# Output weights split during the value projection and kept in DRAM in parts; zero matmuls first, first tokens in halves on two queues

## The chip, the core and the metric

The kernel runs on one core of a Trainium2 chip. TensorE (PE) multiplies, ScalarE (ACT) and VectorE (DVE) work on tiles, GpSimd (POOL) does a few masks and starts some transfers, SyncE (SP) starts most transfers. The metric is the device time of one execution in microseconds, the median of three timed runs. 0.2% of it is 2.1 us.

## The reference

One layer of a decoder on 1024 tokens of width 1024, all in float32, where `P`, `q`, `k`, `v` and `f` are column groups of one projection:

```python
h = x @ w_in                                   # columns [pool 512 | q 512 | k 512 | v 512 | gate 8]
pool = scale * GroupLinear(TrailingMean_w(u) - u)        # 4 groups of 128 channels, w = 2, 4, 8, 16
attn = softmax(q k^T / 8 + c_t - c_s, causal) v          # 8 heads of 64, c = cumsum(log sigmoid(f + b_f))
x = LayerNorm(alpha * x + concat(pool, attn) @ w_out)    # w_out is 1024 x 1024
x = LayerNorm(alpha * x + relu(x @ w_mlp1)**2 @ w_mlp2)  # hidden width 4096
```

## The kernel before

Every float32 operand of a product is kept as two parts: `hi`, a copy rounded to the type that PE multiplies in one pass (a CAST on ACT, line 71), and `lo`, what the rounding left (a subtraction on DVE, line 72). `split` (lines 70 to 72) makes both. A product is three matmuls, hi by hi, hi by lo and lo by hi (`three`, lines 83 to 85).

The program is one straight list for each engine; every engine takes its own list in order, and a planner that works with estimated durations sets that order when the program is built. Buffers are slots of five pools in on-chip memory (S for raw input, Q and A for general use, B for long-lived operands, U for small ones), and a slot that is taken again waits for its last reader. On-chip sums lie in eight banks named `s`, `pt`, `pv` and `mm`. A transfer is started by the engine in whose list it stands; if it has to wait, all that stands behind it on that engine waits too.

The stages in order of time:

- Value projection, to about 54 us. x comes transposed: `load_x(c, kp)` loads and splits 256 input channels of token half c. `load_wvf(kp)` does the same for the value and gate weights. For the first 512 tokens the loop runs over the eight channel blocks k outside and over 8 banks inside, so PE starts as soon as block 0 is there; for the second 512 tokens each of 8 (token tile, column half) pairs runs over all k. `vf_out` copies a finished bank out (line 157 on ACT, 158 and 160 on DVE).
- Pooling and query/key projections from the same x tiles (`load_w`, `proj`, `pool_group`, `qk_proj`), then attention over 8 heads in 4 pairs (`att_probs`, `att_values`). The next pair's projection is fed into attention piece by piece as filler; in the last pair the filler is pooling group 0 (`last_fill`), whose result goes through a DRAM scratch `mix_dram`, as the heads' results do.
- Output projection from about 315 us: `wout` is loaded to S slots and split into B slots (the loop before `load_row`, line 482), which come free when the x tiles are done, that is, while the last pair of heads runs. Its other operand is read back from `mix_dram` (line 750).
- Layer norm, the two products of the MLP with a two-level Strassen scheme, layer norm.

Of the kernel before, what the change touches and what calls it, by code (L numbers as in the profile page):

```python
# [8 lines left out]
F32 = mybir.dt.float32  # L9
# [5 lines left out]
P = 128  # L15
# [21 lines left out]
def trunk(ctx, tc, xT, xn, wuqk, wvf, bf, poolw, pscale, wout, g1, b1, w1, w2, g2, b2, out):  # L37
# [70 lines left out]


    xs = {}  # L110

    def load_x(c, kp):
        st = slot("Q" if c == 0 else "S", [2, CH], F32)
        for k in range(2):
            if c == 0 and kp == 0:
                nc.sync.dma_start(st[:, k], xT[c, kp, :, k])
            elif k == 0:
                nc.sync.dma_start(st, xT[c, kp])
            if k == 0:
                x = slot("B", [2, 2, CH])  # L120
            t = x[:, k]
            split(t[:, 0], t[:, 1], st[:, k])
            xs[c, 2 * kp + k] = t

    wv = []

    def load_wvf(kp):
        st = slot("S", [2, 2 * VW], F32)
        hi, lo = slot("A", [2, 2 * VW]), slot("A", [2, 2 * VW])
        wv.append((hi, lo))  # L130
        if kp:
            nc.sync.dma_start(st, wvf[kp])
        for k in range(2):
            pieces = [slice(0, VW), slice(VW, 2 * VW)] if kp == 0 and k == 0 else [slice(0, 2 * VW)]
            for c in pieces:
                if kp == 0:
                    nc.sync.dma_start(st[:, k, c], wvf[kp, :, k, c])
                split(hi[:, k, c], lo[:, k, c], st[:, k, c])
                yield
# [21 lines left out]

    for kp in range(4):
        g = load_wvf(kp)
        if kp == 0:
            next(g)
        load_x(0, kp)
        for _ in g:
            pass
    nc.sync.dma_start(bf_sb, bf)
    nc.sync.dma_start(ps_sb, pscale)  # L170
    acc0 = []
    for t in range(4):
        acc0.append(tuple(bank()[:, 0:VW] for _ in range(2)))
# [7 lines left out]
    for kp in range(4):  # L181
        load_x(1, kp)
    for t in range(4, NT):
        for half in range(2):
            b = bank()[:, 0:VW]
            for k in range(KT):
                vf_mm(t, half, b, k)
            vf_out(t, half, b)

# [288 lines left out]
    for kp in range(KT // 2):  # L478
        hi, lo = slot("B", [2, D]), slot("B", [2, D])
        for k in range(2):  # L480
            st = slot("S", [D], F32)
            nc.sync.dma_start(st, wout[2 * kp + k])
            split(hi[:, k], lo[:, k], st)
            wo.append((hi[:, k], lo[:, k]))
# [667 lines left out]
```

## Time and profile before

| | us |
|---|---|
| three timed runs | 1046.09, 1044.00, 1045.35 |
| their median | 1045.35 |
| the profiled execution, whole | 1042.84 |
| its span, first to last instruction | 1041.1 |
| PE busy in the span | 1014.8 |
| DVE busy | 760.5 |
| ACT busy | 510.1 |

PE is busy for 97% of the span; the other engines have room on average. What stays is to ask where PE is not busy, or busy and slow, and which instruction ended each wait. Times below are counted from the span's start.

### The profile page before, as it was taken

The page shows a single profiled execution, that of the slowest core. Times are in us where ns is not written, and L with a number is a line of the kernel's source. Part 1 is how long each engine was busy: PE and PEld are TensorE (multiplying, and loading weights), DVE is VectorE, ACT ScalarE, POOL GpSimd, SP SyncE. Part 2 cuts the span into 40 slices and gives each one's busy share as a digit, 9 for nine tenths or more (in the row PEclk, how much of TensorE's full clock was granted, in tenths as well). Part 3 has the DMA queues.
Part 4 walks back from the last instruction along what each step waited for, and adds up shares of the span by engine and source line. Part 5 has one row for each costly group of instructions (what it writes and reads, how often), then busy time and mean ns, then how long its engine had stood idle before and what let it go on. Part 6 is the DMA issues. An engine that isn't in the chain of part 4 may idle for free.

```text
span 1041.1 us, 13988 instructions
## 1 busy us (share of the span) xinstructions
PE 1014.8 (97%) x4958; PEld 842.8 (81%) x4958; DVE 760.5 (73%) x1301; ACT 510.1 (49%) x819; POOL 137.2 (13%) x236
## 2 busy tenths in 40 slices
PE   8999999999989999999999999999999999999996
PEld 7988888878767888888888888888788888888885
DVE  4576678777795896989887878788875565566547
ACT  4423566666674331677666766768621121122152
POOL 0000112111000021113112122120100000000047
PEclk9999999999999999999999999999999999999998
DMA  6302311111346542139757667565999888878753
GB/s 224 104 28 82 103 51 52 34 49 55 113 151 178 194 148 95 62 120 362 286 223 272 233 246 279 215 263 188 342 314 312 273 267 285 277 223 272 237 190 122
DMA packets 111798, 195.81 MB, mean 188 GB/s; under 512 B 9256, under 2 KB 77672, under 8 KB 111728
## 3 DMA queue, kind: packets, MB, share of 16 engines
q1 hardware_dynamic: 95600, 136.71, 40.1%
q0 software_dynamic: 15840, 57.68, 14.3%
q8 instruction: 39, 0.64, 0.2%
q10 hardware_dynamic: 288, 0.52, 0.1%
q14 instruction: 31, 0.25, 0.1%
HBM read 127.18 MB, written 67.70 MB: 187 GB/s over the span
## 4 chain that ended last, share of the span: by engine, by line
PE 52%; DVE 5%; DMA 1%; issue 0%; ACT 0%; POOL 0%; DVEq 0%; SPq 0%
PE s L953 15%; PE s L599 9%; PE pv L953 8%; PE pt L599 6%; PE mm L599 6%; PE pv L599 4%; PE pt L953 2%; PE mm L953 2%; DVE B L72 1%; DVE A L722 1%; DMA hid_dram<-A 1%; DMA A<-hid_dram 1%; DVE Q L72 0%; DMA S<-in_w_dram 0%; DVE bns L502 0%
## 5 line engine op out<-in xcount | busy, mean ns | idle before, releaser
L71 ACT CAST B<-S 128x1024 fp32r<-128x1024 f32 (+1 forms) x92 | 78.3, 870 | 171.9 <-DMA S<-in_w_dram 66.4
L72 DVE TENSOR_TENSOR B<-S,B 128x1024 fp32r<-128x1024 f32 (+1 forms) x92 | 90.2, 993 | 35.1 <-ACT B L71 35.0
L599 PE MATMUL s<-B,Q 128*128 128x512 f32 x480 | 113.5, 389 | 0.2 <-ACT B L71 0.2
L599 PEld LDWEIGHTS s<-B,Q 128*128 128x128 f32 x480 | 90.0, 188 | 19.3 <-ACT B L71 0.6
L953 PE MATMUL s<-B,Q 128*128 128x512 f32 x390 | 94.8, 389 | 0.0
L953 PEld LDWEIGHTS s<-B,Q 128*128 128x128 f32 x390 | 73.2, 188 | 15.5
L71 ACT CAST Q<-S 128x1024 fp32r<-128x1024 f32 x52 | 54.5, 1050 | 62.3 <-PE s L599 17.0
L953 PE MATMUL s<-B,A 128*128 128x512 f32 x333 | 83.1, 394 | 1.1 <-DMA A<-hid_dram 1.1
L724 POOL DMA_DIRECT2D hid_dram<-A x90 | 48.3, 541 | 219.0 <-ACT A L721 174.6
L953 PEld LDWEIGHTS s<-B,A 128*128 128x128 f32 x333 | 62.4, 188 | 15.8 <-DMA A<-hid_dram 1.7
L72 DVE TENSOR_TENSOR Q<-S,Q 128x1024 fp32r<-128x1024 f32 x52 | 63.2, 1216 | 12.1 <-ACT Q L71 12.0
L599 PE MATMUL pt<-B,Q 128*128 128x512 f32 x300 | 71.6, 389 | 0.0
L599 PE MATMUL mm<-B,Q 128*128 128x512 f32 x300 | 71.6, 389 | 0.0
L391 PE MATMUL pv<-A,B 128*128 128x256 f32 x320 | 62.8, 298 | 6.7 <-ACT A L376 3.8
L391 PEld LDWEIGHTS pv<-A,B 128*128 128x128 f32 x320 | 49.9, 188 | 22.3 <-ACT A L376 11.1
L599 PEld LDWEIGHTS mm<-B,Q 128*128 128x128 f32 x300 | 56.3, 188 | 11.7
L599 PEld LDWEIGHTS pt<-B,Q 128*128 128x128 f32 x300 | 56.3, 188 | 11.7
L377 DVE TENSOR_TENSOR A<-pt,A 128x512 fp32r<-128x512 f32 (+1 forms) x80 | 49.0, 633 | 15.8 <-ACT A L376 15.3
L355 ACT ACTIVATE A<-A,nm 128x1024 f32<-128x1024 f32 (+7 forms) x64 | 49.7, 776 | 18.8 <-DVE nm L353 17.5
L722 DVE TENSOR_TENSOR A<-A,A 128x1024 f32<-128x1024 f32 x45 | 53.6, 1219 | 0.8 <-ACT A L721 0.8
L340 POOL TENSOR_TENSOR A<-A,maskb 128x128 f32<-128x128 f32 x48 | 22.4, 467 | 232.9 <-DVE nm L353 135.7
L953 PE MATMUL pv<-B,Q 128*128 128x512 f32 x204 | 50.2, 389 | 0.0
(401 smaller groups left out, 2297.9 us busy)
## 6 DMA issues: line engine op xcount, KB each, us to landing
hid_dram<-A POOLq DMA_DIRECT2D x105, 512.0 KB, 4.0
S<-in_w_dram SPq DMA_DIRECT2D x62, 512.0 KB, 3.5
Q<-hid_dram SPq DMA_DIRECT2D x101, 256.0 KB, 4.7
A<-hid_dram SPq DMA_DIRECT2D x79, 256.0 KB, 5.3
S<-in_wuqk_dram SPq DMA_DIRECT2D x12, 512.0 KB, 3.3
A<-ncf_dram SPq DMA_DIRECT2D x8, 512.0 KB, 3.7
S<-in_wout_dram SPq DMA_DIRECT2D x8, 512.0 KB
S<-mix_dram SPq DMA_DIRECT2D x8, 512.0 KB, 5.0
```

The lines of the kernel that those rows point to most:

```text
L71: nc.scalar.copy(hi, src)
L72: nc.vector.tensor_tensor(lo, src, hi.bitcast(F32), ALU.subtract)
L340: nc.gpsimd.tensor_tensor(nb[:, qs], nb[:, qs], maskb, ALU.add)
L355: nc.scalar.activation(pt[:, :nk], pt[:, :nk], AF.Exp, bias=nm, scale=-1.0, accum_out=rsum[h][:, i : i + 1])
L377: nc.vector.tensor_tensor(tt[:, 1, ev], tp[:, ev], tt[:, 0, ev].bitcast(F32), ALU.subtract)
L391: nc.tensor.matmul(ov, V[j][:, h].rearrange("p s d -> p (s d)"), tt[:, s, a:b], start=(j == 0 and s == 0), stop=(j == 2 * m + 1 and s == 1),)
L599: nc.tensor.matmul(dst, b[x][:, k], A[a][y][:, k], start=first and k == 0 and i == 0, stop=k == H - 1 and i == 2, skip_group_check=not first,)
L722: nc.vector.tensor_tensor(x, x, hi.bitcast(F32), ALU.subtract)
L724: nc.gpsimd.dma_start(hid_dram[self.u, :, i, AT[name] : AT[name] + 2 * CH], part.rearrange("p q n t -> p (q n t)"))
L953: nc.tensor.matmul(dst, h[:, p_], w[q_], start=first and u == self.us[0] and j == 0, stop=u == self.us[-1] and j == 2, skip_group_check=no ...
```

## The change

Four things are edited.

- At the start 18 matmuls of 128 by 256 zeros are put ahead of PE's list (they write a bank that the first real product overwrites), after one MEMSET on DVE.
- The first x block is loaded in halves: its first 256 tokens are started from ACT's list, the rest from SP's. The first block of weights is loaded whole instead of in two column pieces, and weights and x now alternate. The loads of the second token half go to Q slots instead of S slots.
- In the value projection of the second token half, each of the 8 steps also loads one 128-row block of `wout`, splits it (CAST on ACT, line 199 of the new program; subtraction on DVE, line 200) and starts two transfers of 512 KB from POOL's list (line 202) that store `hi` and `lo` in a new DRAM scratch `wo_dram`.
- In front of the output projection the 8 loads of `wout` with 8 splits are replaced by 16 loads of the stored parts straight into the B slots (line 509), with no work on ACT or DVE.

```diff
--- before.py
+++ after.py
@@ -106,21 +106,25 @@
     rin_dram = dr.tile([NH, S], F32, name="rin_dram")
     mix_dram = dr.tile([4, P, 8, 256], F32, name="mix_dram")
 
+    wo_dram = dr.tile([KT, 2, P, D], F32, name="wo_dram")
+
 
     xs = {}
 
     def load_x(c, kp):
-        st = slot("Q" if c == 0 else "S", [2, CH], F32)
+        st = slot("Q", [2, CH], F32)
+        x = slot("B", [2, 2, CH])
+        if c or kp:
+            nc.sync.dma_start(st, xT[c, kp])
         for k in range(2):
-            if c == 0 and kp == 0:
-                nc.sync.dma_start(st[:, k], xT[c, kp, :, k])
-            elif k == 0:
-                nc.sync.dma_start(st, xT[c, kp])
-            if k == 0:
-                x = slot("B", [2, 2, CH])
             t = x[:, k]
-            split(t[:, 0], t[:, 1], st[:, k])
             xs[c, 2 * kp + k] = t
+            first = c == kp == k == 0
+            for i, r in enumerate((slice(0, 256), slice(256, CH)) if first else (slice(0, CH),)):
+                if c == kp == 0:
+                    (nc.scalar if first and i == 0 else nc.sync).dma_start(st[:, k, r], xT[c, kp, :, k, r])
+                split(t[:, 0, r], t[:, 1, r], st[:, k, r])
+                yield
 
     wv = []
 
@@ -131,10 +135,9 @@
         if kp:
             nc.sync.dma_start(st, wvf[kp])
         for k in range(2):
-            pieces = [slice(0, VW), slice(VW, 2 * VW)] if kp == 0 and k == 0 else [slice(0, 2 * VW)]
-            for c in pieces:
-                if kp == 0:
-                    nc.sync.dma_start(st[:, k, c], wvf[kp, :, k, c])
+            if kp == 0:
+                nc.sync.dma_start(st[:, k], wvf[kp, :, k])
+            for c in [slice(0, VW), slice(VW, 2 * VW)] if kp == 0 and k == 0 else [slice(0, 2 * VW)]:
                 split(hi[:, k, c], lo[:, k, c], st[:, k, c])
                 yield
 
@@ -159,18 +162,20 @@
         hs = slice(4 * half, 4 * half + 4)
         nc.vector.tensor_tensor(z[:, t, hs], src[:, 4 * HD : VW], bf_sb[:, hs], ALU.add)
 
+
+    acc0 = [tuple(bank()[:, 0:VW] for _ in range(2)) for t in range(4)]
+    zero = slot("Q", [256])
+    nc.vector.memset(zero.bitcast(F32), 0.0)
+    for _ in range(18):
+        nc.tensor.matmul(acc0[3][1][:, 0:256], zero[:, 0:P], zero, start=True, stop=True)
+
     for kp in range(4):
-        g = load_wvf(kp)
-        if kp == 0:
-            next(g)
-        load_x(0, kp)
-        for _ in g:
-            pass
+
+        gw, gx = load_wvf(kp), load_x(0, kp)
+        for g in (gw, gx, gw, gx, gw, gx):
+            next(g, None)
     nc.sync.dma_start(bf_sb, bf)
     nc.sync.dma_start(ps_sb, pscale)
-    acc0 = []
-    for t in range(4):
-        acc0.append(tuple(bank()[:, 0:VW] for _ in range(2)))
     for k in range(KT):
         for t in range(4):
             for half in range(2):
@@ -179,13 +184,35 @@
         for half in range(2):
             vf_out(t, half, acc0[t][half])
     for kp in range(4):
-        load_x(1, kp)
+        for _ in load_x(1, kp):
+            pass
+
+    raw = {}
+
+    def load_output_weights(k):
+        if k < KT:
+            raw[k] = slot("Q", [D], F32)
+            nc.sync.dma_start(raw[k], wout[k])
+
+    def split_output_weights(k):
+        hi, lo = slot("Q", [D]), raw[k]
+        nc.scalar.copy(hi, lo)
+        nc.vector.tensor_tensor(lo, lo, hi.bitcast(F32), ALU.subtract)
+        for i, part in enumerate((hi.bitcast(F32), lo)):
+            nc.gpsimd.dma_start(wo_dram[k, i], part)
+
+    AHEAD = 3
+    for k in range(AHEAD):
+        load_output_weights(k)
     for t in range(4, NT):
         for half in range(2):
             b = bank()[:, 0:VW]
             for k in range(KT):
                 vf_mm(t, half, b, k)
             vf_out(t, half, b)
+            k = 2 * (t - 4) + half
+            load_output_weights(k + AHEAD)
+            split_output_weights(k)
 
 
     zf = z.rearrange("p t h -> p (t h)")
@@ -478,9 +505,8 @@
     for kp in range(KT // 2):
         hi, lo = slot("B", [2, D]), slot("B", [2, D])
         for k in range(2):
-            st = slot("S", [D], F32)
-            nc.sync.dma_start(st, wout[2 * kp + k])
-            split(hi[:, k], lo[:, k], st)
+            for i, part in enumerate((hi, lo)):
+                nc.sync.dma_start(part[:, k].bitcast(F32), wo_dram[2 * kp + k, i])
             wo.append((hi[:, k], lo[:, k]))
 
     def load_row(tag, src):
```

The planner is run anew on the changed program. Its lists are the same as before (but for names) outside three places: the start, the value projection of the second token half, and the last pair of heads up to the first tiles of the output projection.

**PE, program start.** Before, PE's list began with the first product of the value projection (`A` is weights, `B` is x):

```order
L83 MATMUL s_166<-A_100,B_107 128x260 [waits Activation_49]
L84 MATMUL s_166<-A_101,B_107 128x260 [waits DVE_49]
L83 MATMUL s_168<-A_100,B_107 128x260
L85 MATMUL s_166<-A_100,B_107 128x260 [waits DVE_49]
L83 MATMUL pt_167<-A_100,B_107 128x260 [waits Activation_49]
L84 MATMUL s_168<-A_101,B_107 128x260
```

Now it begins with the 18 zero matmuls, and the first four products are hi by hi of two token tiles:

```order
L170 MATMUL mm_107<-Q_108 128x256 [waits DVE_49]
L170 MATMUL mm_107<-Q_108 128x256 x17
L83 MATMUL s_100<-A_129,B_135 128x260 [waits Activation_49]
L83 MATMUL s_102<-A_129,B_135 128x260
L83 MATMUL pt_101<-A_129,B_135 128x260 [waits Activation_49]
L83 MATMUL mm_103<-A_129,B_135 128x260
L84 MATMUL s_100<-A_130,B_135 128x260 [waits DVE_49]
L85 MATMUL s_100<-A_129,B_135 128x260
```

The zero matmuls wait for DVE's MEMSET alone; the first real matmul stands behind all 18.

**ACT, value projection of the second token half.** Before, the bank copies (line 157) followed the last x casts, with the weights of the next projection between them (line 71, `S` source):

```order
L71 CAST B_415<-S_413 128x512 [waits DMAHW0_49]
L71 CAST B_415<-S_413 128x512
L157 CAST B_445<-s_420 128x4x64 [waits PE_49]
L157 CAST B_445<-pt_449 128x4x64 [waits PE_49]
L157 CAST B_445<-s_477 128x4x64 [waits PE_49]
L157 CAST B_445<-mm_505 128x4x64 [waits PE_49]
L157 CAST B_558<-s_533 128x4x64 [waits PE_49]
L71 CAST B_678<-S_676 128x1024 [waits DMAHW1_49]
L71 CAST B_772<-S_770 128x1024 [waits DMAHW2_49]
```

Now seven CASTs of `wout` blocks (line 199) stand among the bank copies (line 160), and the next projection's weights stand behind them; `DMASW` is a wait for an earlier store started by POOL, because `hi` takes the slot that it left:

```order
L199 CAST Q_515<-Q_445 128x1024 [waits DMAHW2_49,DMASW0_49,DVE_49]
L199 CAST Q_550<-Q_447 128x1024 [waits DMAHW3_49,DVE_49]
L199 CAST Q_585<-Q_478 128x1024 [waits DMAHW4_49,DVE_49]
L160 CAST B_474<-s_449 128x4x64 [waits PE_49]
L199 CAST Q_621<-Q_513 128x1024 [waits DMAHW5_49,DMASW2_49,DVE_49]
L160 CAST B_474<-pt_485 128x4x64 [waits PE_49]
L199 CAST Q_654<-Q_548 128x1024 [waits DMASW3_49,DMAHW1_49,DVE_49,Activation_49]
L160 CAST B_474<-s_520 128x4x64 [waits PE_49]
L199 CAST Q_687<-Q_583 128x1024 [waits DMASW4_49,DMAHW2_49,DVE_49,Activation_49]
L199 CAST Q_720<-Q_619 128x1024 [waits DMAHW3_49,DMASW5_49]
L160 CAST B_474<-mm_555 128x4x64 [waits PE_49]
L160 CAST B_615<-s_590 128x4x64 [waits PE_49]
```

The eighth, of block 0, stands further up, ahead of the first bank copy. DVE's list has the eight subtractions in the matching places.

**DVE and SP, last pair of heads.** DVE before, at the end of pooling group 0 (lines 260 and 262, and line 72 with `Q` operands), with a split of `wout` (line 72, `B` from `S`) between:

```order
L260 SCALAR_TENSOR_TENSOR Q_3252<-Q_3249,Q_2935 128x1023 [waits DVE_49]
L262 TENSOR_TENSOR Q_3252<-Q_3252,Q_2935 128x1 [waits DVE_49]
L397 TENSOR_TENSOR U_3297<-pv_3231,U_3297 64x256 [waits DMAHW0_49,Activation_49]
L353 ISA A_3308,nm_3312<-s_3309,A_2862 128x512
L353 ISA nm_3312 128x1
L406 RECIPROCAL ri_3375<-rsum_2928 128x2
L72 TENSOR_TENSOR B_3561<-S_3562,B_3560 128x1024 [waits DMAHW7_49]
L72 TENSOR_TENSOR Q_3257<-Q_3252,Q_3256 128x1024 [waits Activation_49]
```

DVE now, at the same place:

```order
L287 SCALAR_TENSOR_TENSOR Q_3331<-Q_3328,Q_3014 128x1023 [waits DVE_49]
L289 TENSOR_TENSOR Q_3331<-Q_3331,Q_3014 128x1 [waits DVE_49]
L424 TENSOR_TENSOR U_3376<-pv_3310,U_3376 64x256 [waits DMAHW4_49,Activation_49]
L380 ISA A_3387,nm_3397<-s_3393,A_2941,nm_3391 128x384
L380 ISA nm_3397 128x1
L380 ISA A_3400,nm_3404<-s_3401,A_2941 128x512
L380 ISA nm_3404 128x1
L72 TENSOR_TENSOR Q_3336<-Q_3331,Q_3335 128x1024 [waits Activation_49]
```

The split is gone, and a softmax step (line 380) now stands ahead of the pooling group's split. On SP, before, the row of gate sums for the last head (`ncf_dram`, line 324) stood ahead of `wout` loads:

```order
L398 DMA mix_dram<-U_2907 64x256 [waits DMAHW1_49,DVE_49]
L411 DMA rin_dram<-row_2964 8x128 [waits DMAHW2_49,Activation_49]
L324 DMA A_2927<-ncf_dram 128x1024 [waits DMAHW3_49,PE_49]
L482 DMA S_3542<-in_wout_dram 128x1024 [waits DMAHW4_49,DVE_49]
L411 DMA rin_dram<-row_3013 2x128 [waits DMAHW5_49,Activation_49]
L482 DMA S_3546<-in_wout_dram 128x1024 [waits DMAHW6_49,DVE_49]
```

Now two loads of stored parts stand ahead of it (line 351 is the same load of the row):

```order
L425 DMA mix_dram<-U_2921 64x256 [waits DMAHW6_49,DVE_49]
L509 DMA B_3609<-wo_dram 128x1024 [waits DMAHW7_49,DMASW0_49,PE_49]
L509 DMA B_3609<-wo_dram 128x1024 [waits DMAHW0_49,DMASW2_49]
L425 DMA mix_dram<-U_2986 64x256 [waits DMAHW1_49,DVE_49]
L438 DMA rin_dram<-row_3043 8x128 [waits DMAHW2_49,Activation_49]
L351 DMA A_3006<-ncf_dram 128x1024 [waits DMAHW3_49]
L509 DMA B_3610<-wo_dram 128x1024 [waits DMAHW4_49,PE_49]
```

The first of the two waits for PE to release the slot and for POOL's store of that part.

## Rows read from the trace of the kernel before

**Rows 1.** The page, its part 1: busy time of each engine.
```profile
PE 1014.8 (97%) x4958; PEld 842.8 (81%) x4958; DVE 760.5 (73%) x1301; ACT 510.1 (49%) x819; POOL 137.2 (13%) x236
```

**Rows 2.** Busy time by stretch: engines, granted clock, DMA share, GB/s.
```profile
4.60:9.60 5.00, 4.71 (x19) 4.37 (x20) 2.80 (x5) 2.58 (x5) 0.00 (x0) 1.00 0.89 342
270.00:290.00 20.00, 19.69 (x119) 16.22 (x118) 17.88 (x48) 16.56 (x40) 1.25 (x4) 1.00 0.43 146
290.00:310.00 20.00, 15.66 (x96) 12.08 (x94) 18.69 (x42) 14.78 (x29) 0.62 (x2) 1.00 0.40 139
310.00:330.00 20.00, 17.40 (x107) 14.45 (x106) 13.98 (x25) 10.85 (x21) 0.62 (x2) 1.00 0.72 210
470.00:480.00 10.00, 9.67 (x44) 7.69 (x42) 9.79 (x13) 6.53 (x9) 4.32 (x8) 1.00 1.02 379
```

**Rows 3.** Timeline, first 11 us: start, duration, engine, line, operation [idle before, releaser].
```profile
0.74 0.20 POOL masks.py:197 MEMSET ident<- 128x128 f32 x1 [0.29 <-POOLq L1141]
...
4.64 0.59 PE L83 MATMUL s<-A,B 128*128 128x260 f32 x1 [4.64 <-ACT B L71]
...
7.35 0.63 ACT L71 CAST A<-S 128x520 fp32r<-128x520 f32 x1 [1.19 <-DMA S<-in_wvf_dram]
...
9.30 0.38 PE L85 MATMUL pt<-A,B 128*128 128x260 f32 x1
...
9.51 0.29 PE L83 MATMUL pv<-A,B 128*128 128x260 f32 x1
...
9.64 0.28 PE L84 MATMUL pv<-A,B 128*128 128x260 f32 x1
...
10.24 0.28 PE L83 MATMUL s<-A,B 128*128 128x260 f32 x1
```

**Rows 4.** Busy time of PE in the value projection, its two halves.
```profile
4.64:30.41 25.77, 25.51 (x192) 1.00 0.52 196
30.41:54.29 23.88, 23.69 (x194) 1.00 0.34 114
```

**Rows 5.** Groups of instructions from 255 to 310 us, by shape.
```profile
L72 DVE TENSOR_TENSOR B<-S,B 128x1024 fp32r<-128x1024 f32 x8 | 9.7, 1211 | 0.0
...
L71 ACT CAST B<-S 128x1024 fp32r<-128x1024 f32 x8 | 8.4, 1045 | 0.5 <-DMA S<-in_wout_dram 0.5
```

**Rows 6.** Waits of PE from 255 to 345 us.
```profile
PE pv L391 <- ACT A L376: 3.5, 4, 1.4
PE pv L391 <- DVE A L377: 1.9, 3, 1.0
PE mm L83 <- ACT Q L71: 1.3, 1, 1.3
```

**Rows 7.** Timeline, 294 to 316 us.
```profile
295.01 1.22 DVE L72 TENSOR_TENSOR B<-S,B 128x1024 fp32r<-128x1024 f32 x1
...
301.55 1.20 DVE L72 TENSOR_TENSOR B<-S,B 128x1024 fp32r<-128x1024 f32 x1
...
302.67 1.21 DVE L72 TENSOR_TENSOR Q<-Q,Q 128x1024 fp32r<-128x1024 f32 x1
...
303.93 0.50 PE L84 MATMUL mm<-Q,U 128*128 128x512 f32 x1 [0.92 <-DVE Q L72]
...
315.34 0.50 PE L83 MATMUL s<-B,Q 128*128 128x512 f32 x1
```

**Rows 8.** The page, its parts 2 and 6: mean DMA rate, issues to landing.
```profile
DMA packets 111798, 195.81 MB, mean 188 GB/s; under 512 B 9256, under 2 KB 77672, under 8 KB 111728
...
hid_dram<-A POOLq DMA_DIRECT2D x105, 512.0 KB, 4.0
```

**Rows 9.** Timeline, 270 to 278 us.
```profile
273.08 0.34 SPq L324 DMA_DIRECT2D A<-ncf_dram  x1
...
276.92 0.29 DVE L353 CUSTOM_DVE_ANT_0 A<-s,A 128x128 f32<-128x128 f32 x1 [0.15 <-DMA A<-ncf_dram]
```

**Rows 10.** Timeline, 45 to 50 us.
```profile
46.82 2.00 ACT L71 CAST B<-S 128x1024 fp32r<-128x1024 f32 x2
```

## The prediction

> **What bounds the kernel now.** I read the page's busy times first: PE is busy for 1014.8 us of a 1041.1 us span, no other engine above three quarters [rows 1]. So time can only be won where PE stands still, or runs at its lower clock level. The busy times by stretch came second, to find such places near the edits. Two stand out. From 4.6 to 9.6 us PE ran only 19 matmuls; from 290 to 330 us it was busy for 15.66 + 17.40 of 40 us, so 6.9 us idle, with DVE busy for 18.69 of the first 20 us [rows 2]. The timelines of these places came third, then what PE waited for.
>
> At the start PE's first matmul is at 4.64 us. Matmuls of 260 columns follow each other at 0.21 us up to 9.51 us (9.30 to 9.51), and at 0.12 us from there (9.64 to 10.24 is five of them) [rows 3]. 260 columns in 0.21 us is the 1.2 GHz level, in 0.12 us the 2.4 GHz level. So the clock rose 4.9 us after PE began, and channel block 0 took from 4.64 to 10.24 us: 5.6 us, where 24 matmuls at 0.12 us take 2.9. After that PE never starves in the first half: it ends at 30.41 us [rows 4].
>
> Beside this stands the granted clock of the same stretch, 1.00 [rows 2], which would say that PE ran at full speed all along. The Trainium skill ("TensorE: Matmul & The Clock Gate", section "Seeing it yourself") warns that the clock events in a trace have been seen to be unreliable. By the column the zeros could win nothing and would only delay the first product (rival B); by the spacing they win the term below. The spacing is measured on the matmuls themselves, so it decides.
>
> At the end of attention PE waits for ACT's casts of turned probabilities (3.5 us), for DVE's subtractions of them (1.9) and for the split of pooling group 0 (1.3 and, at 303.93, 0.9 us) [rows 6, 7]. The splits of `wout` stand in these two lists: 8 casts of 1.05 us on ACT and 8 subtractions of 1.21 us on DVE between 255 and 310 us [rows 5].
>
> **The change part by part.** The sum is made against the profiled execution, 1042.84 us, of which 1.7 us lie outside the span; it is 2.5 us below the median of 1045.35, and I take the difference over to the median.
>
> *Zeros.* DVE fills the tile as soon as the engines start: 0.74 us, plus at most twice POOL's 0.20 us for half as many elements [rows 3], so PE begins at about 1.2 us. 18 matmuls of 256 columns at 0.21 us are 3.9 us, to 5.1 us. If the clock again rises 4.9 us after PE's first matmul, that is at 6.1 us. Block 0 then runs from 5.1: 5 matmuls slow to 6.1, 19 at 0.12 us, done at 8.4 us instead of 10.24. That is a gain of 1.8 us, if block 1 is there. Its last cast began at 7.35 and took 0.63 us [rows 3], so it was ready at 7.98 with the same 1 MB loaded ahead of it as now; the new alternation of weights and x does not make it later. Bounds: with the clock up at 5.1 us block 1's data is the limit, a gain of 2.3; with no effect of the zeros on the clock a loss of 0.5, since the first product starts at 5.1 instead of 4.64 us.
>
> *Halves on two queues, whole weight block.* About the same bytes have to land before the first product as before, and PE is in the zeros until 5.1 us. Cost and gain nothing beside the zeros. If the cover goes (data later than 5.1 us), each microsecond costs one, up to the 2.5 us or so by which block 1 could slip.
>
> *x of the second half in Q slots.* These loads no longer wait for S slots. The second half of the value projection took 23.88 us [rows 4] where 192 matmuls at 0.12 us are 23.0. I take 0.5 of the 0.9 us, since the first x cast still stands behind the fifth bank copy; bounds -0.3 (one more such wait) and +0.9.
>
> *Splits moved into the value projection.* 8 casts of 1.05 and 8 subtractions of 1.21 us, 8.4 and 9.7 us, now lie between about 20 and 46 us. PE waits for none of them. What stands behind them is the bank copies (each bank is needed again only by the next projection, after 52 us) and the casts of that projection's weights, which ran at 46.82 us before [rows 10] and are needed by about 52. The new waits are ACT's casts that wait for a store from POOL to leave its slot. A store of 512 KB landed 4.0 us after its issue [rows 8]. The last such wait is for the store of block 1's `lo`, issued at about 36.5 us (my estimate: x casts done at about 33, three casts, then DVE), so at about 41 us; only a landing after some 47 us would reach PE. Cost zero, bounds 0 and +3 us if stores run at half that speed with queues. On SP the loads of the next weights stand behind `wout` loads that wait for slots, with the same margin. POOL has nothing else to do here.
>
> *Splits gone from the end of attention.* Here the gain lies on the chain of pooling group 0: its split feeds the products at 303.93 us, whose result goes to DRAM and back before the output projection can begin at 315.34 us [rows 7]. Two `wout` subtractions stand in DVE's list ahead of that split, at 295.01 and 301.55 us, 1.22 and 1.20 us [rows 7]; without them the chain comes 2.4 us sooner, and the output projection with it. I take 2.4 us. What is late next is the latency from transposed probabilities over ACT and DVE back to PE, 3.5 + 1.9 us of waits [rows 6], which shrinks only in part. Bounds: all 6.9 us of idle time, and a loss of 1.4 us, the longest single wait there [rows 6], since the planner set PE's list anew and gives the last heads fewer output matmuls as filler.
>
> *16 loads instead of 8.* 8.4 MB instead of 4.2 MB pass while the last pair of heads runs. 270 to 310 us moved 146 and 139 GB/s, 5.7 MB; now about 10 MB, 250 GB/s, where 470 to 480 us reached 379 GB/s [rows 2]. It fits, with no cost on the sum. Two of these loads stand ahead of the gate-sum row of the last head, which was issued at 273.08 us and for which DVE waited 0.15 us at 276.92 [rows 9]; at 379 GB/s they put it off by up to 2.8 us. DVE has two splits less there, PE was busy for 19.69 of 20 us with filler at hand [rows 2], so I count zero, bound 1.5.
>
> Sum: 1.8 + 0.5 + 2.4 = 4.7 us. 1042.84 - 4.7 = 1038.1 for a profiled execution, 1045.35 - 4.7 = 1040.6 us for the median. After 330 us the lists are unchanged and PE is the bound, so a gain is kept.
>
> **The rivals.**
>
> A. *The end of attention gains nothing.* The chain of pooling group 0 gives way, but the in-order waits for turned probabilities take its place. For it: 5.4 of 7.6 us of waits there are of that kind, and PE gets less filler. Against: the same two engines get 18 us lighter. Time 1045.35 - 2.3 = 1043.05.
>
> B. *The clock does not rise sooner*, because zeros do not count or the granted clock is right. Then 0.5 is lost and 0.5 + 2.4 won: 1045.35 - 2.4 = 1042.9. For it: no row shows PE on zeros. Against: the spacing in the trace.
>
> C. *All idle time at the end of attention goes*: 1.8 + 0.5 + 6.9 = 9.2, so 1036.1. For it: DVE was at 18.69 of 20 us exactly where PE stood. Against: the chain over DRAM stays.
>
> D. *The parts come too late.* From the row at 273.08 us to the first output matmul at 315.34 there are some 40 us for about 10 MB. If the loads, mixed with small ones, run at 200 GB/s, near the mean of 188 over the span [rows 8], they take 50 us, the output projection starts up to 10 us late, and the time is 1045.35 - 2.3 + 10 = 1053. It is slower than before from a rate of about 225 GB/s downward. Against: 342 GB/s were reached from 4.6 to 9.6 us [rows 2].
>
> **How the numbers follow.** Forecast 0.53, A 0.20, B 0.08, C 0.10, D 0.09. 0.2% is 2.1 us, so faster means below 1043.3. The forecast gives 0.50 of its 0.53 to faster, C all of 0.10, A and B lie just at the bound and give 0.16 of 0.28; together 0.76. The same: 0.03 + 0.12 + 0.03 of a mild D = 0.18. Slower: 0.06. The range runs from 1036.5 (most of C left out) to 1044.5 (A and B with a microsecond of loss); what lies outside is D and the end of C.
>
> **What would show it.** In the changed kernel's profile: the spacing of PE's matmuls falls from 0.21 to 0.12 us near 6 us; block 1 starts near 8.4 us; the second half of the value projection starts near 28.5 us and ends near 52; no wait of PE for ACT or DVE between 36 and 60 us; the products of pooling group 0 about 2.4 us earlier than the shift of the start alone gives; idle time of PE from there to the first layer norm near 4.5 us instead of 6.9. Wrong would be: slow spacing up to 9 us or later; a wait of PE for the next projection's weights near 52 us; the first output matmul waiting for a part from DRAM.

## The result and the profile after

The changed kernel takes 1047.38 us (median of 20 runs), the kernel before 1044.98 us on the same chip: a ratio of 1.0029, 95% interval 1.0021 to 1.0038. The ratios in this document are worked out over the single runs and are not the quotients of the medians; one run of the kernel before, of 2618.65 us, is left out of this one. By the medians the change is 2.4 us slower where 4.7 us of gain were forecast, and outside the range of 1036.5 to 1044.5.

The profiled execution of the changed kernel took 1047.44 us, its span 1045.7. The one of before was 2.1 us under its own median, so the two traces lie 4.6 us apart and the medians 2.4; shifts below are between the two traces. First the page's busy times, which answer to [rows 1]:

```profile
PE 1019.1 (97%) x4976; PEld 845.7 (81%) x4976; DVE 760.7 (73%) x1303; ACT 510.3 (49%) x820; POOL 146.3 (14%) x252
```

PE has 18 instructions more, the zeros (PEld is PE's loading of weights, beside its matmuls). Then the busy times by stretch (columns as in [rows 2]):

```profile
4.60:9.60 5.00, 5.00 (x38) 4.87 (x38) 2.94 (x7) 3.22 (x8) 0.00 (x0) 1.00 1.00 352
290.00:310.00 20.00, 18.44 (x114) 14.93 (x113) 15.36 (x41) 11.51 (x26) 0.94 (x3) 1.00 0.75 267
310.00:330.00 20.00, 17.79 (x111) 14.45 (x110) 14.34 (x30) 13.78 (x28) 0.63 (x2) 1.00 0.73 241
40.00:50.00 10.00, 10.00 (x86) 10.00 (x85) 6.82 (x11) 7.57 (x12) 3.77 (x8) 1.00 1.00 398
50.00:60.00 10.00, 10.00 (x55) 8.66 (x55) 3.71 (x9) 0.17 (x1) 0.99 (x2) 1.00 1.01 368
60.00:70.00 10.00, 3.52 (x17) 2.57 (x16) 7.23 (x33) 2.73 (x6) 0.00 (x0) 0.86 0.18 67
70.00:80.00 10.00, 10.00 (x41) 7.84 (x40) 9.38 (x13) 1.77 (x4) 0.00 (x0) 0.80 0.05 15
```

The start, from the timeline of PE, for [rows 3]:

```profile
1.19 4.21 PE L170 MATMUL mm<-Q 128*128 128x256 f32 x18 [1.19 <-DVE Q L168]
...
5.84 0.29 PE L83 MATMUL pt<-A,B 128*128 128x260 f32 x1
5.96 0.28 PE L83 MATMUL mm<-A,B 128*128 128x260 f32 x1
...
8.49 0.28 PE L83 MATMUL s<-A,B 128*128 128x260 f32 x1
```

The zeros run from 1.19 us, the spacing of 260 columns is 0.12 us from 5.84 on, and block 1 begins at 8.49 us (10.24 before). The start and the end of attention went as hoped: 38 matmuls from 4.6 to 9.6 us where there were 19, and 3.8 us idle from 290 to 330 where there were 6.9 [rows 2]. The new thing is between 60 and 70 us: PE is busy for 3.52 of 10 us, and in the next ten its granted clock is 0.80. Ahead of that, from 40 to 60 us, the DMA engines are full (share 1.00 and 1.01), and ACT, which has splits and bank copies to do, is busy for 0.17 of 10 us.

The waits of PE over the whole span name the place (waiting form, line, releaser: us in total, times, longest):

```profile
PE s L248 <- DVE Q L239: 6.5, 1, 6.5
...
PE pv L625 <- DVE A L715: 1.1, 1, 1.1
```

One wait of 6.5 us: the transposes of the gate (L248; the gate is the log sigmoid of `f + b_f`, whose running sum c attention needs) wait for the last step of the gate's arithmetic on DVE (L239). Before, PE did not wait there at all; these are the four steps of that chain before, from the timeline:

```profile
50.30 0.33 SPq L270 DMA_DIRECT2D S<-in_poolw_dram  x1
...
52.80 0.30 ACT L71 CAST U<-S 128x128 fp32r<-128x128 f32 x1 [0.58 <-DMA S<-in_poolw_dram]
...
62.42 0.23 DVE L212 SCALAR_TENSOR_TENSOR Q<-Q 128x64 f32<-128x64 f32 x1
...
65.19 0.60 PE L221 MATMUL s<-ident,Q 128*8 128x128 f32 x4
```

And the same chain after, with what stands around it, from the timeline in order of time:

```profile
46.73 2.19 POOL L202 DMA_DIRECT2D wo_dram<-Q  x4 [0.79 <-DVE Q L200]
47.88 2.35 DVE L200 TENSOR_TENSOR Q<-Q,Q 128x1024 f32<-128x1024 f32 x2
49.40 1.67 POOL L202 DMA_DIRECT2D wo_dram<-Q  x3 [0.48 <-DVE Q L200]
50.55 2.35 DVE L72 TENSOR_TENSOR B<-S,B 128x1024 fp32r<-128x1024 f32 x2
51.80 0.33 SPq L76 DMA_DIRECT2D S<-in_wuqk_dram  x1
52.93 0.56 SPq L297 DMA_DIRECT2D S<-in_poolw_dram  x1
61.29 0.30 ACT L71 CAST U<-S 128x128 fp32r<-128x128 f32 x1 [11.12 <-DMA S<-in_poolw_dram]
61.50 0.37 ACT L160 CAST B<-mm 128x256 fp32r<-128x256 f32 x1
61.63 0.29 DVE L72 TENSOR_TENSOR U<-S,U 128x128 fp32r<-128x128 f32 x1 [7.92 <-ACT U L71]
61.90 0.42 DVE L161 TENSOR_TENSOR B<-mm,B 128x256 fp32r<-128x256 f32 x1
62.42 0.20 DVE L224 TENSOR_SCALAR Q<-z 128x64 f32<-128x64 f32 x1
69.42 0.22 DVE L239 SCALAR_TENSOR_TENSOR Q<-Q 128x64 f32<-128x64 f32 x1
69.79 1.01 PE L248 MATMUL s<-ident,Q 128*8 128x128 f32 x4 [6.49 <-DVE Q L239]
...
71.88 0.63 PE L84 MATMUL s<-B,B 128*128 128x512 f32 x1
72.31 0.63 PE L85 MATMUL s<-B,B 128*128 128x512 f32 x1
```

Read it from the bottom. PE waits for DVE's L239 at 69.42. The gate's 7 us of arithmetic began at 62.42, behind the last bank copy of the value projection (L161), behind the `lo` part of pooling group 3's weights (L72), which waits for its cast on ACT, which had stood idle for 11.12 us, at the end for a load of 64 KB. That load was issued at 52.93 us and used from 61.29 on: 8.4 us, where before it took 2.5 (50.30 to 52.80). Ahead of it, at 46.73 and 49.40, seven stores of `wo_dram` parts had been issued. The load is late for a second reason too: it is issued 2.6 us later than before, although PE is 2.05 us ahead. It goes into an S slot that DVE frees by splitting the next weights (L72 at 50.55), and this now stands behind subtractions of output weights (L200). The products of group 3 themselves are not needed until the attention; the load holds PE up only because ACT and DVE work their lists in order, and the gate stands behind its split.

After the wait PE runs at its 1.2 GHz level: 512 columns every 0.43 us (71.88 to 72.31) until 74.0, with a granted clock of 0.50, then every 0.23. So the wait costs 6.5 us and about 2 us behind it. The page's table of issues shows what full DMA engines do to the stores (KB each, median us from issue to landing; a store of 512 KB by POOL took 4.0 us before [rows 8]):

```profile
wo_dram<-Q POOLq DMA_DIRECT2D x16, 512.0 KB, 7.4
```

Where the 4.6 us between the traces arise, by the start of the same instruction in both (after minus before; each difference is one subtraction of two rows of the timelines):

| place | time before | after minus before |
|---|---|---|
| block 1 of the value projection, PE | 10.24 | -1.75 |
| first product of group 3's pooling projection, PE | 54.29 | -2.05 |
| first transpose of the gate, PE | 65.19 | +4.60 |
| first subtraction of turned probabilities, DVE | 121.33 | +6.64 |
| last residual sum before the MLP, DVE | 414.77 | +3.44 |
| inside the first MLP product, DVE | 570.20 | +4.16 |
| last normalization, DVE | 1035.68 | +4.63 |

Won 2.05 at the start and 3.2 from 121 to 415 us; lost 8.7 between 54 and 121, and 1.2 behind 415.

### The profile page after: what moved, and what is told of

Its sections match the earlier page's. It is cut to its first block, busy times and chain, and to the rows that moved or that the text cites. A ratio compares the mean times of both kernels' runs of the same rounds, so it can differ in the third digit from the quotient of the medians.

```text
span 1045.7 us, 14123 instructions
## 1 busy us (share of the span) xinstructions
PE 1019.1 (97%) x4976; PEld 845.7 (81%) x4976; DVE 760.7 (73%) x1303; ACT 510.3 (49%) x820; POOL 146.3 (14%) x252
## 4 chain that ended last, share of the span: by engine, by line
PE 52%; DVE 4%; DMA 2%; issue 1%; ACT 0%; DVEq 0%; SPq 0%; ACTq 0%
PE s L979 15%; PE s L625 9%; PE pv L979 8%; PE pt L625 6%; PE mm L625 6%; PE pv L625 4%; PE pt L979 2%; DMA S<-in_w_dram 2%; PE mm L979 2%; DMA A<-hid_dram 1%; DVE Q L72 0%; DVE B L72 0%; DVE A L748 0%; DVE bns L528 0%; ACT Q L71 0%
## 5 line engine op out<-in xcount | busy, mean ns | idle before, releaser
L71 ACT CAST B<-S 128x1024 fp32r<-128x1024 f32 (+1 forms) x76 | 65.7, 877 | 170.5 <-PE s L979 70.6
L72 DVE TENSOR_TENSOR B<-S,B 128x1024 fp32r<-128x1024 f32 (+1 forms) x76 | 75.7, 1004 | 27.1 <-ACT B L71 26.9
L72 DVE TENSOR_TENSOR Q<-S,Q 128x1024 fp32r<-128x1024 f32 x52 | 63.3, 1218 | 15.2 <-ACT Q L71 15.0
L403 ACT CAST A<-pt 128x512 fp32r<-128x512 f32 (+1 forms) x80 | 41.7, 539 | 18.3 <-PE pt L402 17.1
```

Source lines behind the costliest of these rows:

```text
L71: nc.scalar.copy(hi, src)
L72: nc.vector.tensor_tensor(lo, src, hi.bitcast(F32), ALU.subtract)
L403: nc.scalar.copy(tt[:, 0, ev], tp[:, ev])
```

## The experiments

Theory 1: the small load of group 3's pooling weights shares the DMA engines with the stores of the parts, lands some 6 us later after its issue, and through ACT's and DVE's in-order lists holds up the gate and PE; the forecast gains at both ends are there. The rivals are named in each expectation. "Before" is always the kernel before on the same chip in the same series of runs; intervals are 95%.

**One load moved (`poolw_early`).** In the changed kernel:

```
+    pw_raw = slot("U", [P], F32)                     # behind ps_sb's load
+    nc.sync.dma_start(pw_raw, poolw[:, EARLY[0]])
...
+        st = pw_raw                                  # in pool_linear, for EARLY[0]
```

> The changed kernel with one load moved: the weights of pooling group 3 (64 KB) are loaded into a U slot right behind the forget bias and the pool scale, long before the first store of a part. TensorE's list is unchanged. Theory 1 (the small load stands behind the stores and holds up the last bank copy, the gate and so TensorE): the 6.5 us wait of the gate's transposes goes, and with it the 2.0 us that the following matmuls lost at the 1.2 GHz level; the end of attention keeps its gain. 1047.4 - 6.5 - 2.0 = 1038.9 us, between 1038 and 1041. Rival 1 (ACT's and DVE's lists are late by themselves there, through casts that wait for a store to leave a Q slot): the gate starts only a little earlier, at most 2 us come back, 1045.4 to 1047.4. Rival 2 (the next weights in line, loaded at 51.8 us in the changed kernel, are late just as much): the wait moves to the projection behind and about half comes back, 1043 us.

Measured: 1040.05 us against 1044.01, ratio 0.9968 (0.9957 to 0.9980): faster than before. Moving 64 KB turns 2.4 us of loss into 4.0 us of gain. The planner moved the cast and the subtraction of these weights along with the load, out of the bank copies' way. PE's waits no longer show the gate; the transposes run at full speed:

```profile
30.05 0.39 PE L83 MATMUL s<-A,B 128*128 128x260 f32 x1 [0.98 <-ACT B L71]
...
64.12 0.60 PE L250 MATMUL s<-ident,Q 128*8 128x128 f32 x4
```

Rival 2 falls, and rival 1 as the whole cause. The first row is a side effect: the planner moved one of ACT's casts of x behind three bank copies (the expectation of `poolw_v4` says four), and 0.98 us of the start's gain went there.

**The same load on another queue (`poolw_act_queue`).** Rival 3 was that the load only stood behind the 512 KB issued on SP just ahead of it:

```
-        nc.sync.dma_start(st, poolw[:, g])
+        (nc.scalar if g == EARLY[0] else nc.sync).dma_start(st, poolw[:, g])
```

> The changed kernel with one edit: the same small load of group 3's weights is issued by ACT instead of SP, at the same place (after DVE has freed the S slot, near 53 us). TensorE's list is unchanged. Theory 1 in the form that the DMA engines themselves are full with stores, whatever queue a load comes by: it still lands near 60 us, TensorE still waits 5 to 6.5 us, the time is that of the changed kernel within 1 us (1046.4 to 1048.4). Rival 3 (the load is late because it stands behind 512 KB of the next weights in SP's own queue): it lands within 3 us, the wait goes, 1039 to 1041 us.

Measured: 1047.22 us, ratio 1.0043 (1.0028 to 1.0059). From the timeline:

```profile
52.33 0.34 ACTq L297 DMA_DIRECT2D S<-in_poolw_dram  x1
60.06 0.30 ACT L71 CAST U<-S 128x128 fp32r<-128x128 f32 x1 [6.99 <-DMA S<-in_poolw_dram]
...
68.55 1.01 PE L248 MATMUL s<-ident,Q 128*8 128x128 f32 x4 [5.36 <-DVE Q L239]
```

With nothing ahead of it in ACT's queue it still took 7.7 us, and PE waited 5.4. So the load shares the engines with the stores, and its place in SP's queue does not explain the delay. The Trainium skill says of transfers started by ScalarE, SyncE or GpSimd that they run on the same 16 DMA engines and interleave, whichever of the three started them ("DMA: Bandwidth & Descriptors", section "Issuing engines are not separate DMA queues"). This run agrees, with 7.7 us from ACT's queue against 8.4 from SP's.

**The first part of the change alone (`start_only`).** Zeros, halves and Q slots as in the changed kernel, `wo_dram` and its loops taken out, the splits at the end of attention as before.

> Before plus the first part of the change alone: zeros, the first tokens by halves on two queues, x in Q slots; the output weights are split at the end of attention as before. Theory 1: the 2.05 us won by the end of the value projection are kept to the end, 1045.0 - 2.05 = 1042.9 us (1042.2 to 1043.7), the gate waits for nothing, and TensorE waits at the end of attention as before. Rival 4 (the earlier start is itself to blame, as TensorE comes to the gate's transposes sooner and waits there): a wait of up to 2 us at those transposes, 1045.

Measured: 1041.76 us against 1044.01, ratio 0.9982 (0.9973 to 0.9991). The gate's transposes are at 63.24 us, 1.95 before those of before, with no wait; the small load took 2.9 us from issue (48.34) to its cast (51.24). The time fell a little below the expected stretch, the gain of 2.25 us against the forecast's 2.3 for these terms. Rival 4 falls.

**The second part alone (`parts_only`).** `raw`, the two functions, `AHEAD` and the loads of parts put into the kernel before, whose start stays.

> Before plus the second part of the change alone: output weights split during the value projection and kept in DRAM in parts; the start as before. Theory 1: the wait at the gate's transposes is there too, about 4.5 to 6.5 us as TensorE comes there 2 us later, and costs about 2 us of clock behind it; the end of attention gives 3 us back, later waits take 1: 1045.0 + 5.5 + 2.0 - 3.2 + 1 = 1050.3 us (1048 to 1052). Rival 4 (the earlier start makes the wait): no wait above 1 us, 1042.

Measured: 1050.02 us, ratio 1.0064 (1.0050 to 1.0079): the expected number, but not by the expected wait. PE's waits:

```profile
PE s L83 <- ACT B L71: 11.5, 2, 6.5
```

(the other of the two is the start, as before) and ACT's timeline where that wait ends:

```profile
44.35 1.14 ACT L71 CAST B<-S 128x512 fp32r<-128x512 f32 x2 [1.36 <-DMA S<-in_xT_dram]
```

Here the planner put all eight loads of output weights ahead of the last block of x on SP (issued at 35.22 us), so PE starved for x. The gate did not wait, and the small load took 2.8 us (60.15 to 62.96). It suggests that the moved splits need the Q slots for x, but as the whole start is as before, it does not single them out. It doesn't test the gate: that my sum met the time is chance.

**The load early, the casts of x in place (`poolw_v4`).** The same two added lines as in `poolw_early`, but ahead of `zf = ...`, which leaves ACT's casts of x where the changed kernel has them.

> As poolw_early, but the early load of group 3's weights stands behind the first five output-weight loads on SP, and the planner keeps ACT's casts of the second half's x where the changed kernel has them (in poolw_early one of them moved behind four bank copies, and TensorE waited 0.98 us for it at 30.05 us). TensorE's list is unchanged. Theory 1 with that reading: no wait at the gate's transposes, and the 0.98 us go too: poolw_early's 1040.05 - 0.9 = 1039.1 us (1038.5 to 1039.8). Rival: the load, now issued near 18 us beside other transfers, or the cast, comes late again and TensorE waits: 1040 or more.

Measured: 1038.82 us against 1043.82, ratio 0.9953 (0.9939 to 0.9967). This is the best version: 5.0 us under the kernel before, and close to the 4.7 that were forecast for the change. The gate's transposes are at 63.10 us with no wait. The moved splits still cost DVE time here: the gate's arithmetic ends at 62.05 us, where it ended at 60.69 in `start_only`, which leaves PE a margin of 1.0 us.

**The zeros taken away (`no_zeros`).** `poolw_v4` without `zero`, its memset and the 18 matmuls; the planner also sets a few instructions of ACT and DVE near 34 and 45 us in another order.

> poolw_v4 without the 18 zero matmuls (their tile and its memset are gone too), all else the same. Forecast's term: TensorE begins near 4.6 us at the 1.2 GHz level and the clock rises near 9.5, so 1.8 us are lost, poolw_v4 + 1.8 = 1040.9 us (1040.5 to 1041.4). Rival B (zeros do not count for the clock): 0.5 us faster than poolw_v4, 1038.6.

Measured: 1041.19 us, ratio 0.9976 (0.9965 to 0.9987); 2.4 us above `poolw_v4`, in the traces 2.22 (gate's transposes at 65.32 and 63.10). PE's timeline without zeros:

```profile
5.17 0.58 PE L83 MATMUL s<-A,B 128*128 128x260 f32 x1 [5.17 <-ACT A L71]
...
9.98 0.42 PE L83 MATMUL mm<-A,B 128*128 128x260 f32 x1
10.20 0.42 PE L84 MATMUL mm<-A,B 128*128 128x260 f32 x1
...
10.85 0.30 PE L84 MATMUL s<-A,B 128*128 128x260 f32 x1
10.98 0.28 PE L85 MATMUL s<-A,B 128*128 128x260 f32 x1
```

260 columns every 0.22 us at 10.2, 0.13 at 10.85: the clock rose some 5.6 us after PE began; with zeros it was up at 5.84 us. Rival B falls. The halves and the whole weight block do cost something: the first product comes at 5.17 us instead of 4.64 [rows 3], which the zeros hide.

**Half the stored bytes (`lo_only`).**

```
-        for i, part in enumerate((hi.bitcast(F32), lo)):
-            nc.gpsimd.dma_start(wo_dram[k, i], part)
+        nc.gpsimd.dma_start(wo_dram[k, 1], lo)
...
+            st = slot("S", [D], F32)                  # at the end of attention
+            nc.sync.dma_start(st, wout[2 * kp + k])
+            nc.scalar.copy(hi[:, k], st)
+            nc.sync.dma_start(lo[:, k].bitcast(F32), wo_dram[2 * kp + k, 1])
```

> The changed kernel with half the stored bytes: only the lo part of each block goes to DRAM (8 stores, 4.2 MB instead of 8.4); at the end of attention hi is cast by ACT from the raw weights again, lo is loaded. The load of group 3's weights stays where the changed kernel has it. Theory 1: with 4.2 MB less at about 400 GB/s the train of stores ends some 10 us sooner, near 50 us; the small load lands within 3 us of its issue, the gate's transposes wait for less than 0.5 us, the clock stays up; the end of attention gives back about 1 of its 3 us for ACT's eight casts: 1047.4 - 6.5 - 2.0 + 1 = 1039.9 us (1039 to 1042). Rival (it is not the amount of stored bytes that holds the load): the wait stays above 4 us, 1046 to 1048.

Measured: 1040.10 us, ratio 0.9966 (0.9956 to 0.9976). The small load took 3.2 us (issued at 48.46, cast at 51.65) and PE did not wait. It was also issued 4.5 us sooner, because DVE, less held up, freed the S slot sooner; so the run halves the train and its delay together.

**The stores and nothing else (`stores_alone`).** `start_only` plus 16 stores whose data nobody reads:

```
+            if half == 1 and t in (5, 6):
+                for k in range(8):
+                    nc.gpsimd.dma_start(spare_dram[4 * (t - 5) + k // 2, k % 2], V[t]...)
```

> start_only (1041.8 us, no output-weight part moved) plus nothing but 16 stores of 512 KB by POOL, of finished values into a spare DRAM tensor that nobody reads: 8 when the values of token tile 5 are done (near 40 us), 8 after tile 6 (near 46 us). The lists of TensorE, ACT, DVE and SP are those of start_only. Theory 1 (stores alone are enough: the 16 DMA engines are full and the small load of group 3's weights, issued near 48.3 us, comes out only with the end of the train): 8.4 MB at 400 GB/s from 40 us last to about 61; the load lands between 57 and 61 us instead of 51.2, TensorE waits 3.5 to 7 us at the gate's transposes and loses 1 to 2 us of clock behind: 1046 to 1050 us. Rival 1 (it takes the splits and their waits for Q slots in ACT's and DVE's lists): no wait, 1041.8 within 1 us.

Measured: 1046.35 us, ratio 1.0022 (1.0013 to 1.0031); 4.6 us above `start_only` (measured in another series), with PE's, ACT's, DVE's and SP's lists the same. From the timeline:

```profile
43.42 4.42 POOL L213 DMA_DIRECT2D spare_dram<-B  x8 [41.21 <-DVE B L161]
...
48.66 0.67 SPq L295 DMA_DIRECT2D S<-in_poolw_dram  x1
...
58.17 0.30 ACT L71 CAST U<-S 128x128 fp32r<-128x128 f32 x1 [7.59 <-DMA S<-in_poolw_dram]
...
66.68 0.97 PE L246 MATMUL s<-ident,Q 128*8 128x128 f32 x4 [2.96 <-DVE Q L237]
```

Stores alone are enough for a late load (9.5 us from issue to use), a wait and the low clock behind it. The load was there at 58, as expected, but not with the end of the train: the engines were full to 70 (share 0.97 from 60 to 70 us). So the load gets a share of the engines; it does not stand behind every store.

The wait of 2.96 us is under the expected 3.5 to 7, and less than half of the changed kernel's 6.49. The rest is the second reason: here the load is issued at 48.66 us, in the changed kernel at 52.93, since DVE's added subtractions free its S slot 4.3 us later. In the changed kernel it then takes 1.1 us less, and PE comes to the transposes 0.4 us sooner (63.30 and 63.72), which makes up the 3.5 us between the two waits. The late issue alone would cost little, by an estimate from these rows: issued at 52.93 and used after 2.9 us as in `start_only`, with the transposes ready 8.5 us later (61.29 to 69.79), it comes to a wait of 1.0 us. No run tests that.

**The wait filled with products (`gap_products`).** 28 products into a spare bank, which nobody reads, between group 3's projection and `gate_sum`:

```
+            for _ in range(28):
+                nc.tensor.matmul(spare, x[:, 0, 0:P], x[:, 0], start=True, stop=True)
```

> The changed kernel with 28 products into a spare bank, whose result nobody reads, put into TensorE's list between group 3's projection and the gate's transposes: 28 x 0.227 = 6.4 us, the length of the wait. ACT's, DVE's and SP's lists are unchanged. Theory 1 with the clock: the transposes still come near 69.8 us, but at 0.60 us each group instead of 1.01, and the nine matmuls behind them follow each other at 0.23 instead of 0.43 us: 1047.4 - 2.0 = 1045.4 us (1044.9 to 1046.0). Rival (those 2 us are lost to late weights or to DVE, not to the clock): the slow spacing stays and so does the time, 1047.4.

```profile
63.44 6.51 PE L315 MATMUL pv<-B 128*128 128x512 f32 x28
69.79 0.60 PE L248 MATMUL s<-ident,Q 128*8 128x128 f32 x4
...
70.89 0.39 PE L84 MATMUL s<-B,B 128*128 128x512 f32 x1
71.12 0.39 PE L85 MATMUL s<-B,B 128*128 128x512 f32 x1
```

The transposes come at 69.79 as in the changed kernel, and from there on all is at full speed: at 121 us the shift is +4.60 instead of +6.64, so the clock's part is 2.04 us. Of these 1.4 are left at the end of the trace (+3.26 instead of +4.63). The time is 1046.43 us, 0.4 above the expected stretch, ratio 1.0024 (1.0015 to 1.0032), which overlaps the changed kernel's 1.0021 to 1.0038: the place is shown by the trace, the gain of the whole is not told apart by the runs.

**The gate's transposes later (`gate_later`).** `if g == EARLY[0]: gate_sum(neglog)` becomes `EARLY[1]`.

> The changed kernel with the gate's transposes and sum put one pooling group later in TensorE's list (behind group 2's products); the late load of group 3's weights stays. If only the transposes' place in TensorE's list is to blame (they are the one consumer that comes too early): the wait goes, about 1039.5 us. Theory 1 in its full form (ACT's and DVE's in-order lists stand still, so everything behind the late load is late): the lo part of group 2's weights stands behind the gate in DVE's list and is ready near 71.9 us only; TensorE's wait moves to the first product with that lo part, 5 to 7 us, the clock falls again, and the time stays within 1.5 us of the changed kernel, 1046 to 1048.5.

Measured: 1040.52 us, ratio 0.9961 (0.9949 to 0.9973). My expectation was wrong. ACT's cast still waits 11.33 us and DVE is as late as before, but PE goes on:

```profile
61.17 0.30 ACT L71 CAST U<-S 128x128 fp32r<-128x128 f32 x1 [11.33 <-DMA S<-in_poolw_dram]
...
62.81 0.39 PE L83 MATMUL s<-B,B 128*128 128x512 f32 x1
...
73.69 0.60 PE L248 MATMUL s<-ident,Q 128*8 128x128 f32 x4
```

Group 2's weights had been split at 47 to 53 us, ahead of the late load; what I took for theirs was group 1's. So the stand of the two lists has one consumer that feels it, the transposes, and 10 us more of distance are enough.

## Why the prediction was wrong

**The step that failed** is "Splits moved into the value projection ... Cost zero, bounds 0 and +3 us". It cost 8.5 of the 8.7 us lost there: 6.5 of wait and 2.0 of clock. Its bound of +3 was for stores at half speed; they came near that (7.4 us instead of 4.0), and the cost was nearly three times the bound. The step counted the eight casts and subtractions and asked when the last slot would come free; for the bytes it asked only how long a store takes. It did not sum them: 8.4 MB of stores, besides 4.2 MB of loads, at the 398 GB/s that the stretch then ran at are 32 us of full engines, in a stretch where before the engines were used for 0.34 of the time [rows 4]. Nor did it list what else is loaded there, or all that stands behind the bank copies: it wrote that each bank is "needed again only by the next projection, after 52 us", but copying a bank out also gives the gate its input `z`. It named SP's "loads of the next weights" with their margin, and meant the 512 KB ones; the 64 KB load behind them, with a margin of 2.5 us at the gate (62.65 to 65.19 in the chain of before), stood in the trace. Its term for slow stores, "only a landing after some 47 us would reach PE", looked at the stores' own slots alone; the other slot that mattered, the small load's, came free 4.6 us later than in `start_only` (52.93 and 48.34). The sign it named, no wait of PE "between 36 and 60 us", held, and its stretch ended 3.3 us ahead of the wait. `poolw_early`, `poolw_act_queue` and `stores_alone` show the place, the sharing, and that stores are enough for 2.96 of the 6.5 us; that the rest comes from the late issue is read from the traces and was not tested by itself.

**Zeros, 1.8 us.** Right in kind: block 1 starts at 8.49 us (forecast 8.4), the clock is up at 5.84 (forecast 6.1). By `no_zeros` they are worth 2.2 us, since the loads in halves put the first product off by 0.5 us, which I had at nothing; it is hidden as the step said.

**x in Q slots, 0.5 us.** In `no_zeros` the first product is 0.53 us later than before and the gate's transposes 0.13, so about 0.4 us are won. Right. That these slots may also be what keeps x ahead of the new loads (`parts_only`) I had not seen.

**Splits gone from the end of attention, 2.4 us.** The size was right: 3.2 us from 121 to 415 us in the changed kernel, 2.6 in `poolw_v4` (shift -2.09, then -4.69), against 0.2 in `start_only`. The reason was not, so that the size was nearly met is luck. Pooling group 0's split comes at 309.04 us where it was at 302.67 [rows 7]: 6.4 us later, as everything at 271 us (+6.44); no 2.4 us sooner. The output projection begins at 322.33 us where it was at 315.34, 7.0 us later, so the gain comes behind both places that the step named. What went are the waits for turned probabilities: from 255 to 345 us

```profile
PE s L374 <- DVE nm L380: 1.2, 1, 1.2
...
PE pv L418 <- DVE A L404: 0.8, 2, 0.5
...
PE pv L418 <- ACT A L403: 0.4, 2, 0.2
```

where ACT's casts had 3.5 and DVE's subtractions 1.9 us [rows 6]; of these kinds 0.7 us more is left at the line of the transposes (L402). That is the part of which I wrote that it "shrinks only in part". So the 5.0 us of `poolw_v4` beside the 4.7 forecast do not confirm the sum term by term.

**16 loads instead of 8, nothing.** Right: no wait of PE for a part, rival D did not come, with 267 and 241 GB/s from 290 to 330 us.

**"After 330 us the lists are unchanged and PE is the bound, so a gain is kept."** Not quite: behind 415 us 1.2 us went in the changed kernel, 0.9 in `start_only`. Near 480 us PE waits 1.1 us for DVE (L715) instead of 0.3. There ACT waits 2.31 us for 512 KB of weights where before it waited 0.68, and DVE stands behind it. The engines are full there too (404 and 420 GB/s in the halves of 470 to 480 us in `start_only`). All nine traces with the zeros show 1.1 to 1.3 us of this wait, the three without them 0.2 to 0.4; whether the zeros are the reason, and how they could reach a load 470 us later, is open, and wasn't tried. The other 0.5 us of the 1.2 go near 756 us, where PE waits for a load of `hid_dram` for 1.60 us instead of 1.11. At this wait single traces differ by more: in those of `lo_only`, `parts_only` and `stores_alone` (1.64 to 1.79 us of wait) the matmuls behind it follow each other at 0.43 instead of 0.23 us and some 2 us are lost. These three traces lie 2.1 to 2.4 us above the medians of their own kernels, so one trace can carry 2 us that the median does not.

## What to carry to other kernels

When a change adds transfers to a stretch, add up its bytes against the rate the engines reach, and list every other load that is issued inside it, the smallest first: 64 KB beside full engines took 8 us instead of 2.5, and it matters not what the load is for but what stands behind its first use in the lists of that engine. Ask too when the load can be issued: work added to the engine that frees its slot put it off by another 4 us. The repair is then cheap: issue the small load ahead of the train (5.0 us under the kernel before), or move the one consumer of what is late (3.1 us).
When a gain forecast at one end is lost elsewhere, take one trace apart by shifts of the same instruction: the four numbers -2.05, +6.64, +3.44, +4.63 said in one table where to look.

## What was not expected of the hardware

- A 64 KB load beside full DMA engines took 7.7 to 9.5 us from its issue to the cast that uses it, on SP's or ACT's queue (52.33 to 60.06, 52.93 to 61.29, 48.66 to 58.17). Where they were busy for about half of the time (share 0.58 from 50 to 53 us before, 0.50 from 48 to 52 us in `start_only`) it took 2.5 and 2.9 us.
- One wait in a dense stream of matmuls brought PE to its low level, after 6.49 us and also after 2.96: four transposes then took 1.01 and 0.97 us instead of 0.60. The gap of 6.5 us filled with products of no use left it at the high one, which is worth 2.04 us. Shorter waits did either: near 755 us one of 1.60 us in the changed kernel left PE at its high level (granted clock 1.00 from 756 to 760 us), one of 1.79 us in `stores_alone` was followed by the low one (0.60 from 755.7 to 760 us).
